# Gate units of attention in the first phase, output units of the convolution in the second: one decoder layer on one core

## The chip, the core and the metric

The kernel runs on one core of a Trainium2 chip. The core's engines work side by side, each through its own list of instructions in order: TensorE (PE, with PEld for its weight loads), VectorE (DVE), ScalarE (ACT), GpSimd (POOL) and SyncE (SP), which here only issues DMAs. An engine whose next instruction waits on a semaphore does nothing of what is queued behind it. The metric is the device time of one execution in microseconds.

## The reference

A decoder layer on 1024 tokens of width 1024 with two branches, all in float32. With h the normed and modulated input:

```python
proj = h @ w_in
(glu_a, glu_b, z_conv, q, k, v, z_att, g_conv, g_att) = jnp.split(proj, split_idx, axis=-1)

u = glu_a * sigmoid(glu_b)
u = causal_depthwise_conv(u, conv_w) + conv_b            # 31 taps, 1024 channels
u = silu(layernorm(u, conv_ln_g, conv_ln_b))             # over the channels
y_conv = (u * silu(z_conv)) @ w_conv_out

att = merged_dilated_window_attention(rope(q), rope(k), v)   # 3 groups of 8 heads
y_att = (att * silu(z_att)) @ w_att_out

merged = sigmoid(g_conv) * y_conv + sigmoid(g_att) * y_att
x = rmsnorm(x + gate * (merged @ w_o), final_g)
```

## The kernel before

Everything is kept transposed: 128 channels on the partitions, 1024 tokens along the free dimension; a whole such tile is 512 KB. A float32 product is made of three products of rounded parts (`mm3`, L72): each operand is split into a high part (ACT copy to fp32r) and a low part (a subtraction, mostly on POOL). `hh` and `hl` hold the parts of h for all eight channel tiles. A *unit* is 128 output columns of a weight matrix: 8 channel tiles x 2 token halves x 3 = 48 matmuls of 512 columns, done in four groups of 12.

**First phase (L400 to L1091).** A list `groups` holds one function of 12 matmuls per step. Beside it `todo` holds, for each step, the smaller jobs by rank: EARLY, COPY, EVICT, HIGH, POOLED, POST_, LOAD. The loop from L1060 writes out the instructions step by step in that order: EARLY, the group, ACT's work (COPY, EVICT, HIGH), POOL's, DVE's evictions (POST_), then `pump(GROUP)`, then what is left, DMA loads among it. `pump` gives 2.72 credits a step, at most 5.44 kept, to the generators in `behind`, DVE's long chains; each `yield` says what the piece just written costs (`GROUP, TAP, POST = 2.72, 1.33, 0.76`), and `spend` takes DVE's evictions off the same credit. This fixes the order in each engine's list; semaphores fix the times.

The steps before: 0 to 3 a plain unit, 4 to 19 v's second group (`values`), 20 to 131 sixteen *pairs*: two units as one Strassen product (`strassen`, L703) in seven groups instead of eight, with sums formed on POOL and, at its end, two sums on DVE (`summed`). Ten of the pairs are gates that go to scratch in DRAM after their activation (`Stored`). Then 132 to 147 v's third group in two turns, 148 to 155 the first two output units of the convolution together (`first_outputs`), and 156 to 179 the other six (`output`). A weight form of step s is copied by ACT at step s - 3 (`Form`, HIGH) and completed by POOL at step s - 2.

On DVE the depthwise convolution runs beside this, 31 taps for each of eight channel tiles (`conv`), each result stored to `vcscr`. Behind the last tap come the mean over channels by a matmul with ones (`norm_mean`), the squares (`norm_squares`), their column sums on PE and the reciprocal roots (`sums`, `scales`), the row of them by transposes (`rows`), then `norm_apply`: normalising, Silu, product with the stored gate z (`szscr`), and the split of u into parts `ch`, `cl`, which the output units read. The eight channel tiles `vt` stay in SBUF from the squares on. Then the rotation tables (`tables`), `ctab` and `stab`; the row sums of `w_ada` for the residual gate (`gate_sum`) lie between. `Gated` multiplies each output by the stored `gcscr` into `cscr`.

**Second phase (L1094 to L1607).** A loop over slots: each takes half of the contraction of a projection, 12 matmuls (`pieces`), beside stages of attention. 24 units are keys and queries (slots -11 to 84), rotated with the tables as they leave PSUM; then eight units of g_att, slots 85 to 116, which ACT copies out to `ascr` (`gate`). Attention's stages lie in slots 0 to 99, its merge (`combine`) up to slot 114. PSUM has two banks for the projections.

**Third phase.** For each d, `gates_load` reads `ascr` and `cscr`, ACT takes the Sigmoid of the first, and the output of attention is multiplied and added; the final product and norm follow.

Of the kernel before, what the change touches and what calls it, by code (L numbers as in the profile page):

```python
# [39 lines left out]
def layer(ctx: ExitStack, tc: tile.TileContext, a, out):  # L40
# [61 lines left out]
    vcscr = [dram.tile([P, S], F32, name=f"vcscr{j}") for j in range(KT)]  # L102
    szscr = [dram.tile([P, S], F32, name=f"szscr{j}") for j in range(KT)]
# [657 lines left out]
    ch, cl = [None] * KT, [None] * KT  # L761
    vt = [None] * KT
    row_of_mean = []

    def v_loads(cts):
        for ct in cts:
            vt[ct] = slot(f"t{ct}", f"vt{ct}")
            nc.sync.dma_start(vt[ct], vcscr[ct])
# [7 lines left out]

    def norm_squares():
        pm = row_of_mean[0]
        v_loads((KT - 1,))
        tot2 = slot("n2", "tot2")  # L780
        last = None
        for ct in range(KT):
            nc.vector.scalar_tensor_tensor(vt[ct], pm, -1.0 / D, vt[ct], op0=mult, op1=add)
            yield TAP
            sq = conv_in("sq")[:, 0:S] if ct else tot2
            nc.scalar.activation(sq, vt[ct], AF.Square)
            if last is not None:
                nc.vector.tensor_add(tot2, tot2, last)  # L788
# [3 lines left out]
        nc.vector.tensor_add(tot2, tot2, last)  # L792
        yield TAP

        def sums():
            pc = bank()[:, 0:8]
            col_sums(pc, tot2)
            at(now[0], POST_, lambda: scales(pc))
        at(now[0] + 1, EARLY, sums)

    def scales(pc):
        lcols = rstd_cols(pc, "l")
        nc.scalar.activation(one_b[:, 0:1], ones[:, 0:1], AF.Silu)

        def rows():
            lrow = acc_tile("lrow")
            for t in range(8):
                nc.tensor.transpose(lrow[:, t * P:(t + 1) * P], lcols[:, t:t + 1].to_broadcast([P, P]), ident)
            behind.append(norm_apply(lrow))
        at(now[0] + 1, EARLY, rows)  # L810

    sz_t = {}

    def sz_load(ct):
        sz_t[ct] = conv_in("sz")[:, 0:S] if ct % 4 < 2 else slot(f"n{1 + ct % 4}", "sz")
        nc.sync.dma_start(sz_t[ct], szscr[ct])

    def norm_apply(lrow):
        for ct in range(4):
            sz_load(ct)  # L820
        sg = [bank() for _ in range(2)]

        def scaled_mul(ct):
            nc.vector.tensor_mul(vt[ct], vt[ct], lrow)

        def scaled_(ct):
            scaled_mul(ct)
            silu(ct)

        def silu(ct):  # L830
            for half in range(2):
                nc.scalar.activation(sg[half], vt[ct][:, wide(half)], AF.Silu, scale=cvec[:, 1, ct:ct + 1],
                                     bias=cvec[:, 2, ct:ct + 1])

        scaled_(0)
        yield TAP
        for ct in range(KT):
            if ct + 1 < KT:
                scaled_mul(ct + 1)
                yield TAP  # L840
            for half in range(2):
                s = wide(half)
                nc.vector.tensor_mul(vt[ct][:, s], sg[half], sz_t[ct][:, s])
            yield 2 * POST
            if ct + 1 < KT:
                silu(ct + 1)
            hi, lo = slot(f"t{8 + ct}", f"uh{ct}", F32R), slot(f"t{ct - 1}" if ct else "n2", f"ul{ct}", F32R)
            nc.scalar.activation(hi, vt[ct], AF.Copy)
            ch[ct], cl[ct] = hi, lo
            at(now[0] + 1, POOLED, lambda ct=ct: nc.gpsimd.tensor_sub(cl[ct], vt[ct], ch[ct].bitcast(F32)))  # L850
            if ct + 4 < KT:
                sz_load(ct + 4)
# [7 lines left out]
    def tables():  # L860
        ctab, stab = (tabs[0].tile([P, S], F32, name=x) for x in ("ctab", "stab"))
        tabs.extend((ctab, stab))
        posi = pb.tile([P, S], I32, name="posi", tag="sd0")
        nc.sync.dma_start(posi, a["positions"].to_broadcast([P, S]))
        yield GROUP
        n_ = slot("sd1", "n_")
# [26 lines left out]
        yield from wrapped_sin(stab, slot("sd0", "m_"))  # L893
# [8 lines left out]
    class Gated:  # L902


        def __init__(self, step, d):
            self.d = d
            at(step, LOAD, self.load)

        def load(self):
            self.sg = slot(f"n{3 + self.d % 2}", "sgc")  # L910
            nc.sync.dma_start(self.sg, gcscr[self.d])

        def out(self, half, ps):
            y = piece("gs", "gs", 4)
            nc.vector.tensor_mul(y, ps, self.sg[:, wide(half)])
            spend(POST)
            nc.sync.dma_start(cscr[self.d][:, wide(half)], y)

    def gate_sum(step, d):
        box = []  # L920

        def load():
            box.append(slot("t7", "wada"))
# [7 lines left out]

    def u_block(kh, half):
        s = wide(half)
        return lambda k: (ch[4 * kh + k][:, s], cl[4 * kh + k][:, s])

    def first_outputs(step):
        raws = [Raw(step - 7 + 2 * d, a["w_co"][d]) for d in range(2)]
        forms = {(d, kh): Form(step + kh, raws[d].half(kh)) for kh in range(2) for d in range(2)}
        out = [Gated(step + 5, d) for d in range(2)]
        for d in range(KT):  # L940
            gate_sum(step + 7 + 3 * d, d)
        ps = {}

        def group(k):
            def fn():
                for d in range(2):
                    f = forms[d, k // 4]
                    c = slice(k % 4 * P, k % 4 * P + P)
                    for half in range(2):
                        if k == 0:  # L950
                            ps[d, half] = bank()
                        mm3(ps[d, half], f.hi[:, c], f.lo[:, c], ch[k][:, wide(half)], cl[k][:, wide(half)],
                            k == 0, k == KT - 1)
                if k == KT - 1:
                    for d in range(2):
                        for half in range(2):
                            at(now[0], POST_, lambda d=d, half=half: out[d].out(half, ps[d, half]))
            return fn
        return [group(k) for k in range(KT)]

    def output(step, d):
        raw = Raw(step - 6, a["w_co"][d])
        forms = [Form(step + 2 * i, raw.half(i)) for i in range(2)]
        out = Gated(step, d)
        ps = {}

        def group(i, half):
            def fn():
                if i == 0:
                    ps[half] = bank()  # L970
                block(ps[half], forms[i], u_block(i, half), i == 0, i == 1)
                if i:
# [785 lines left out]
```

## Time and profile before

| what | value |
| --- | --- |
| three runs | 1207.67, 1208.96, 1209.08 us; median 1208.96 |
| the profiled execution | 1208.01 us |
| its span, first to last instruction | 1206.2 us, granted clock 0.996 |
| DVE, ACT, POOL busy | 905.1, 586.7, 429.2 us |
| read from HBM, written | 122.25 MB, 39.62 MB |

How to read the views: a row of the groups gives line, engine, operation, output<-input with shape and count, then busy time and mean of one, then the idle time before it with what released it. A row of the order of time gives start and duration. A row of stretches gives for each engine the busy time and, in brackets, the number of instructions. An idle time matters only on the engine that sets the end.

### The profile page before, as it was taken

What the parts mean: (1) busy time and instruction counts of PE and PEld (TensorE: products, weight loads), DVE (VectorE), ACT (ScalarE), POOL (GpSimd) and SP (SyncE); (2) the same over time, 40 slices, a digit from 0 to 9 for tenths busy, and PEclk for the clock granted to TensorE, in tenths of its full rate; (3) what the DMA queues carried; (4) which work ended last, traced back from release to release, by engine and by line L of the source; (5) the groups of instructions that cost most, each with busy time, mean ns of one, the idle gap of its engine ahead of it and who ended that gap; (6) DMA issues with size and microseconds to landing.
All of it is one profiled execution on the core that took longest, in us unless ns stands there. A gap on an engine that the chain in (4) does not pass through costs nothing.

```text
span 1206.2 us, 17336 instructions
## 1 busy us (share of the span) xinstructions
PE 1189.1 (99%) x6042; PEld 996.1 (83%) x6042; DVE 905.1 (75%) x1488; ACT 586.7 (49%) x1213; POOL 429.2 (36%) x316
## 2 busy tenths in 40 slices
PE   9999999999999999999999999999999999999997
PEld 7787888888888888788888888888888888888886
DVE  7879999999999998796346657867877852649444
ACT  5655244545444443741126656656656664445111
POOL 0005867787787874672321111111111111200000
PEclk9999999999999999999999999999999999999999
DMA  9685333313233147666855455665666563768232
GB/s 358 192 300 175 105 106 122 101 66 105 100 100 131 63 140 274 226 201 235 225 135 149 111 144 130 181 174 141 180 168 146 145 191 124 234 228 281 87 105 70
DMA packets 100141, 194.49 MB, mean 161 GB/s; under 512 B 29587, under 2 KB 43219, under 8 KB 100054
## 3 DMA queue, kind: packets, MB, share of 16 engines
q1 hardware_dynamic: 83376, 186.77, 50.4%
q10 hardware_dynamic: 16678, 6.61, 2.0%
q8 instruction: 48, 0.79, 0.3%
q14 instruction: 39, 0.32, 0.1%
HBM read 122.25 MB, written 39.62 MB: 134 GB/s over the span
## 4 chain that ended last, share of the span: by engine, by line
PE 90%; DVE 3%; ACT 2%; DMA 2%; issue 1%; POOL 1%; SPq 0%; DVEq 0%; ACTq 0%; POOLq 0%
PE d L73 23%; PE d L74 23%; PE d L75 23%; PE o L1370 4%; PE d L603 4%; PE s L1333 3%; PE t L1349 3%; PE d L1661 2%; PE d L1662 2%; PE d L1663 2%; DMA wraw<-in_w_v 1%; PE d L274 1%; ACT hh L238 1%; DVE hl L241 1%; DVE tot L788 1%
## 5 line engine op out<-in xcount | busy, mean ns | idle before, releaser
L545 DVE SCALAR_TENSOR_TENSOR acc<-u,cw,acc 128x1024 f32<-128x1024 f32 x232 | 298.8, 1288 | 6.6
L73 PE MATMUL d<-hh,whi 128*128 128x512 f32 x752 | 295.0, 392 | 2.2 <-ACT gs L1023 2.2
L74 PE MATMUL d<-hl,whi 128*128 128x512 f32 x752 | 293.4, 390 | 0.0
L75 PE MATMUL d<-hh,wlo 128*128 128x512 f32 x752 | 293.3, 390 | 0.0
L456 POOL TENSOR_TENSOR wlo<-wraw,whi 128x512 fp32r<-128x512 f32 x130 | 175.8, 1362 | 216.4 <-ACT whi L453 216.2
L58 POOL TENSOR_TENSOR wlo<-wraw,whi 128x512 fp32r<-128x512 f32 (+1 forms) x56 | 82.9, 1498 | 366.5 <-ACT whi L57 362.5
L75 PEld LDWEIGHTS d<-hh,wlo 128*128 128x128 f32 x752 | 141.2, 188 | 30.2
L73 PEld LDWEIGHTS d<-hh,whi 128*128 128x128 f32 x752 | 141.4, 188 | 29.1 <-ACT gs L1023 2.7
L74 PEld LDWEIGHTS d<-hl,whi 128*128 128x128 f32 x752 | 141.4, 188 | 25.9
L453 ACT ACTIVATE whi<-wraw 128x512 fp32r<-128x512 f32 x130 | 79.1, 624 | 86.9 <-DMA wraw<-in_w_co 26.1
L1342 ACT ACTIVATE sb<-sb,stats 128x128 f32<-128x128 f32 (+1 forms) x192 | 84.8, 443 | 31.2 <-DVE stats L1338 30.9
L1338 DVE CUSTOM_DVE_ANT_0 sb<-s,mask 128x128 f32<-128x128 f32 (+1 forms) x192 | 59.7, 349 | 52.9 <-PE s L1333 51.5
L1349 PE MATMUL t<-ident,sb 128*128 128x128 f32 x280 | 73.7, 276 | 0.0
L1370 PE MATMUL o<-ph,vt 128*64 128x128 f32 (+1 forms) x432 | 65.9, 253 | 0.0
L1164 ACT ACTIVATE ph<-t 128x384 fp32r<-128x384 f32 (+2 forms) x96 | 45.6, 475 | 38.9 <-PE t L1349 25.8
L1167 DVE TENSOR_TENSOR pl<-t,ph 128x384 fp32r<-128x384 f32 (+2 forms) x96 | 52.0, 541 | 10.8 <-ACT ph L1164 10.2
L1333 PE MATMUL s<-k,ql 128*128 128x128 f32 (+1 forms) x192 | 55.0, 292 | 0.0
L1164 ACT ACTIVATE kqp<-rot 128x512 fp32r<-128x512 f32 x24 | 23.1, 964 | 64.4 <-DVE rot L1187 39.0
L1370 PE MATMUL o<-pl,vt 128*64 128x128 f32 (+1 forms) x216 | 52.8, 261 | 0.0
L1661 PE MATMUL d<-oh,hh 128*128 128x512 f32 (+1 forms) x136 | 51.2, 377 | 0.0
L1663 PE MATMUL d<-oh,hl 128*128 128x512 f32 (+1 forms) x136 | 51.2, 377 | 0.0
L73 PE MATMUL d<-uh,whi 128*128 128x512 f32 x128 | 50.0, 390 | 1.2 <-ACT gs L612 1.2
(300 smaller groups left out, 2640.2 us busy)
## 6 DMA issues: line engine op xcount, KB each, us to landing
wraw<-in_w_t SPq DMA_DIRECT2D x67, 512.0 KB, 4.2
k<-kqp SPq DMA_DIRECT2D x96, 128.0 KB, 2.3
q<-kqp SPq DMA_DIRECT2D x96, 128.0 KB, 2.3
wraw<-in_w_v SPq DMA_DIRECT2D x19, 512.0 KB, 4.5
wa<-in_w_ada SPq DMA_DIRECT2D x16, 512.0 KB, 5.8
ql<-kqp SPq DMA_DIRECT2D x48, 128.0 KB, 2.3
wg<-wscr SPq DMA_DIRECT2D x48, 128.0 KB, 3.2
hscr<-x SPq DMA_DIRECT2D x8, 512.0 KB, 3.4
```

Source lines behind the costliest of these rows:

```text
L58: (lo_eng or nc.vector).tensor_sub(lo, raw, hi.bitcast(F32))
L73: nc.tensor.matmul(ps, lh, rh, start=start, stop=False, skip_group_check=again)
L74: nc.tensor.matmul(ps, lh, rl, start=False, stop=False, skip_group_check=again)
L75: nc.tensor.matmul(ps, ll, rh, start=False, stop=stop, skip_group_check=again)
L453: nc.scalar.activation(self.hi, src(), AF.Copy)
L456: nc.gpsimd.tensor_sub(self.lo, src(), self.hi.bitcast(F32))
L545: nc.vector.scalar_tensor_tensor(acc, u[:, k:k + S], cw[:, ct, k:k + 1], acc, op0=mult, op1=add)
L1333: products.append((w, lambda c=c, w=w, l=x[:, ts_], r=k[:, ks], i=i: nc.tensor.matmul(ps[:, c:c + w], l, r, start=i == 0, stop=i == 1)))
L1342: nc.scalar.activation(sb[:, c:c + w], sb[:, c:c + w], AF.Exp, bias=stats[:, t, h, 1:2], scale=-1.0, accum_out=stats[:, t, h, 0:1])
L1349: yield from ((lambda c=c: nc.tensor.transpose(ps[:, c:c + P], sb[:, c:c + P], ident)) for c in range(0, o, P))
L1370: nc.tensor.matmul(out_, l, r, **kw))
L1661: nc.tensor.matmul(ps, hh[:, k, c], rh, start=k == 0, stop=False)
```

## The change

Attention's eight gate units become four Strassen pairs more (`GA`) in the first phase, steps 132 to 159, with their Sigmoid at once; v's third group moves to steps 160 to 175, and there the phase ends. The convolution's eight output units leave the first phase and take the gates' slots in the second, reading u from `hh` and `hl`, into which it is brought back from new scratch `uscr` once keys and queries have been projected. Because the Strassen tiles now stay in SBUF longer, the norm no longer keeps its channel tiles: `norm_squares` and `norm_apply` load them again. The core of the diff:

```diff
+    uscr = dram.tile([KT, P, S], F32, name="uscr")
...
+    def less_mean(v):
+        nc.vector.scalar_tensor_tensor(v, row_of_mean[0], -1.0 / D, v, op0=mult, op1=add)
+
+    def written_whole(step, ps):
+
+        at(step, EARLY, lambda: nc.tensor.matmul(ps, hh[:, 0, 0:P], hh[:, 0, 0:512], start=True, stop=True))
+
     def norm_squares():
-        pm = row_of_mean[0]
-        v_loads((KT - 1,))
+        d = {}
+
+        def load(ct):
+            d[ct] = conv_in("d")[:, 0:S] if ct % 3 < 2 else slot("n3", "d")
+            nc.sync.dma_start(d[ct], vcscr[ct])
+
+        for ct in range(3):
+            load(ct)
         tot2 = slot("n2", "tot2")
-        last = None
-        for ct in range(KT):
-            nc.vector.scalar_tensor_tensor(vt[ct], pm, -1.0 / D, vt[ct], op0=mult, op1=add)
+        yield 2 * GROUP
+
+        def square(ct):
+            less_mean(d[ct])
+            nc.scalar.activation(d[ct] if ct else tot2, d[ct], AF.Square)
+
+        square(0)
+        yield TAP
+        for ct in range(1, KT):
+            square(ct)
             yield TAP
...
+            if ct > 1:
+                nc.vector.tensor_add(tot2, tot2, d[ct - 1])
                 yield TAP
-            last = sq if ct else None
+            if ct + 2 < KT:
+                load(ct + 2)
...
-        at(now[0] + 1, EARLY, sums)
+        at(now[0] + 3, EARLY, sums)
...
         def rows():
-            lrow = acc_tile("lrow")
-            for t in range(8):
-                nc.tensor.transpose(lrow[:, t * P:(t + 1) * P], lcols[:, t:t + 1].to_broadcast([P, P]), ident)
+            lrow = slot("n4", "lrow")
+            for half in range(2):
+                pr = bank()
+                for t in range(4):
+                    nc.tensor.transpose(pr[:, t * P:(t + 1) * P],
+                                        lcols[:, 4 * half + t:4 * half + t + 1].to_broadcast([P, P]), ident)
+                nc.scalar.activation(lrow[:, wide(half)], pr, AF.Copy)
+                written_whole(now[0] + 1, pr)
             behind.append(norm_apply(lrow))
-        at(now[0] + 1, EARLY, rows)
+        at(now[0] + 2, EARLY, rows)
...
     def norm_apply(lrow):
...
+        v, z = {}, {}
+
+        def load(ct):
+            v[ct], z[ct] = conv_in("v")[:, 0:S], slot(f"n{2 + ct % 2}", "sz")
+            nc.sync.dma_start(v[ct], vcscr[ct])
+            nc.sync.dma_start(z[ct], szscr[ct])
+
+        def normed(ct):
+            less_mean(v[ct])
+            nc.vector.tensor_mul(v[ct], v[ct], lrow)
+            nc.scalar.activation(v[ct], v[ct], AF.Silu, scale=cvec[:, 1, ct:ct + 1], bias=cvec[:, 2, ct:ct + 1])
+
+        load(0)
+        load(1)
+        yield 2 * GROUP
+        normed(0)
+        yield 2 * TAP
         for ct in range(KT):
             if ct + 1 < KT:
-                scaled_mul(ct + 1)
-                yield TAP
...
+                normed(ct + 1)
+                yield 2 * TAP
+            nc.vector.tensor_mul(v[ct], v[ct], z[ct])
+            nc.sync.dma_start(uscr[ct], v[ct])
+            if ct + 2 < KT:
+                load(ct + 2)
+            yield TAP
...
     def gate_sum(step, d):
...
-            box.append(slot("t7", "wada"))
+            box.append(slot(f"t{d % 2}", "wada"))
...
+    GA = lambda n: stored_pair(60 + 2 * n, [ascr[2 * n], ascr[2 * n + 1]], S_[1])
     for make, n in ((glu_pair, 2), (SZ, 0), (glu_pair, 3), (SZ, 1), (glu_pair, 4), (ZA, 0), (glu_pair, 5), (ZA, 1),
-                    (SZ, 2), (glu_pair, 6), (GC, 0), (SZ, 3), (glu_pair, 7), (GC, 1), (GC, 2), (GC, 3)):
+                    (SZ, 2), (glu_pair, 6), (GC, 0), (SZ, 3), (glu_pair, 7), (GC, 1), (GC, 2), (GC, 3),
+                    *((GA, n) for n in range(4))):
         make(n)
-    at(len(groups), LOAD, lambda: v_loads(range(KT - 1)))
+    at(len(groups) + 1, LOAD, cb_load)
+    for d in range(KT):
+        gate_sum(len(groups) + 4 + d, d)
     for turn in range(2):
         take(values(len(groups), 2, turn))
-    at(len(groups) - 12, LOAD, cb_load)
-    take(first_outputs(len(groups)))
-    for d in range(2, KT):
-        take(output(len(groups), d))
...
-    def gate(d):
...
+    def gated(d, s):
+        y = ap_.tile([P, 512], F32, name="gc", tag="gs", bufs=2)
+        nc.sync.dma_start(y, gcscr[d][:, s])
+
+        def consume(ps):
+            nc.vector.tensor_mul(y, ps, y)
+            nc.scalar.dma_start(cscr[d][:, s], y)
         return consume
...
+        later = {0: ((prepare, kq + 1),), 1: ((raw_for, kq + 2),), 3: ((prepare, kq + 2), (raw_for, kq + 3))}
+        for n, (d, half) in enumerate([(0, 0), (1, 0), (0, 1), (1, 1)] + [(d, h) for d in range(2, KT) for h in range(2)]):
...
+    def u_back(kh, half):
+
+        for c in range(2):
+            k0 = 4 * kh + 2 * c
+            s = slice(half * 512, half * 512 + 512)
+            raw = tabs[0].tile([P, 2, 512], F32, name="u", tag=("ctab", "stab")[c])
+            nc.sync.dma_start(raw, uscr[k0:k0 + 2, :, s].rearrange("k p s -> p k s"))
+            raws["u", c] = raw
+        yield
+        for c in range(2):
+            k0 = 4 * kh + 2 * c
+            hi, lo, raw = hh[:, k0:k0 + 2, s], hl[:, k0:k0 + 2, s], raws["u", c]
+            nc.scalar.activation(hi, raw, AF.Copy)
+            (nc.vector if c else nc.gpsimd).tensor_sub(lo, raw, hi.bitcast(F32))
+        yield
...
+    for n, (kh, half) in enumerate(((0, 0), (1, 0), (0, 1), (1, 1))):
+        in_steps(u_back(kh, half), [80 + 2 * n, 82 + 2 * n])
...
         nc.sync.dma_start(sg_, ascr[d])
-        nc.scalar.activation(sg_, sg_, AF.Sigmoid)
         nc.sync.dma_start(tt, cscr[d])
```

`conv_in` has two buffers, the slots `n2`, `n3`, `n4` one each. `in_steps` runs a generator's first part (the load) at the first slot named and its second (the split) at the other. The table generator works in `ctab` itself and in `n2`, `n3` where it had slots of its own.

More of the change, by code (lines that the diff above doesn't have):

```diff
@@ L892, in tables @@
         yield from wrapped_sin(ctab, n_)
-        yield from wrapped_sin(stab, slot("sd0", "m_"))
+        yield from wrapped_sin(stab, slot("n3", "m_"))
         at(now[0] + 2, POST_, lambda: nc.vector.tensor_scalar(stab, stab, fr[:, 1:2], None, op0=mult))
@@ L930, in gate_sum @@
         at(step, POST_, post)
[L932 to L972, printed above, removed]
-                    at(now[0], POST_, lambda: out.out(half, ps[half]))
-            return fn
-        return [group(i, half) for i in range(2) for half in range(2)]
     groups = []
@@ L1596, in layer @@
                 next(c)
[L1597 to L1598 removed]
+            for do, u in prepared:
+                if u < units:
+                    do(u)
             if 0 <= slot_ < stages and st_ == 7:
```

105 lines of the change are left out of this document (29 added, 76 removed).

## The prediction

> **What bounds the kernel now.** I read the page first, then a table of stretches, then the two ends of the stretch that the change rewrites in TensorE's (PE's) order of time.
>
> ```profile
> span 1206.2 us, 17336 instructions
> ...
> PE 1189.1 (99%) x6042; PEld 996.1 (83%) x6042; DVE 905.1 (75%) x1488; ACT 586.7 (49%) x1213; POOL 429.2 (36%) x316
> ```
>
> PE is busy for 1189.1 of 1206.2 us, so time can fall only by giving PE less work or fewer waits, and any new wait of PE is added whole. The stretches (us; busy time of PE, PEld, DVE, ACT, POOL; granted clock; DMA) are: the block pairs of the first phase, its tail up to the first output of the convolution, the convolution's output units, and the second phase with attention.
>
> ```profile
> 99.00:459.00 360.00, 359.79 (x1584) 297.34 (x1585) 343.91 (x300) 157.99 (x266) 273.12 (x205) 1.00 0.33 108
> 459.00:510.90 51.90, 50.09 (x221) 40.30 (x219) 41.06 (x42) 30.64 (x47) 27.90 (x19) 0.97 0.73 263
> 510.90:598.80 87.90, 87.66 (x384) 72.03 (x385) 57.60 (x73) 25.29 (x37) 42.22 (x24) 1.00 0.70 230
> 598.80:1071.00 472.20, 472.20 (x2869) 407.85 (x2868) 304.06 (x803) 269.77 (x715) 80.90 (x60) 1.00 0.60 155
> ```
>
> PE is filled in all but the second, 459.0 to 510.9: there it lost time, and the clock was 0.97. That is where the layer norm of the convolution lies. In the pairs' stretch POOL is busy for 273 of 360 us and DVE for 344: four pairs more find room on POOL, and on DVE they come after its taps. PE's order of time (start, duration):
>
> ```profile
> 459.03 0.39 PE L603 MATMUL d<-whi,hh 128*128 128x512 f32 x1
> 459.26 0.39 PE L603 MATMUL d<-wlo,hh 128*128 128x512 f32 x1
> ...
> 472.63 1.88 PE L773 MATMUL pm<-tot,ones 128*128 128x512 f32 x4
> ```
>
> ```profile
> 510.91 0.50 PE L73 MATMUL d<-uh,whi 128*128 128x512 f32 x1 [1.22 <-ACT gs L612]
> ```
>
> ```profile
> 598.82 0.39 PE L73 MATMUL d<-hh,whi 128*128 128x512 f32 x1
> ```
>
> Starts are 0.227 us apart (459.26 less 459.03), though one row lasts 0.39: matmuls overlap, and the spacing is the price. One step of the first phase, 12 matmuls, is 2.72 us. Step 132 starts at 459.03 with v's last units; the mean of the norm (L773) comes five steps later, at step 137. Sixteen steps at 2.72 would end at 502.6; the first output unit started at 510.91, 8.4 us later, and the second phase at 598.82.
>
> **The change, part by part.**
>
> *Matmuls.* Step count of the first phase: 32 steps of output units go (8 of the first two, 24 of the rest), 28 steps of gate units come (four pairs of seven). The second phase keeps 32 units of 48 matmuls. PE saves 4 x 12 x 0.227 = **10.9 us**. Three filler matmuls (`written_whole`) add 0.7; the 4 + 4 transposes are the same eight as before. Of the 8.4 us lost in v's last units the mean's 1.9 (L773) stays, with sums and transposes at about 3.3 (my estimate); the rest could go, because more steps now lie between the norm's stages. Were that all, the phase would end 14.2 us earlier: 459.03 + 44 x 2.72 + 5.9 = 584.6.
>
> *The norm's first half* (`norm_squares`) now reloads v through three buffers. A reload waits for the sum two operations back, so a channel costs half of load, handover and two DVE operations (rows below): (3.7 + 0.3 + 2.4) / 2 = 3.2. Eight channels from 478 end near 504; the column sums come at step 149, 459.03 + 17 x 2.72 + 1.9 = 507.2. Hidden, with 3 us of cover; with loads of 5.1 it would be 1 us late.
>
> *The norm's second half.* Before, eight whole channels `vt` stayed in SBUF. Now `norm_apply` has two buffers for v and two for z, and each channel goes: load, less mean, times lrow, Silu, times z, store to `uscr`. Its order on DVE is normed(ct+1), then the product of ct, then the store of ct, then load(ct+2) into the buffer that this store reads. Load(ct+2) must therefore wait until the store of ct has landed, normed(ct+2) for that load, and the product of ct+1 stands behind normed(ct+2) on DVE. The chain runs through **every** channel, not every second one. That SP holds back a load until a store has landed shows here (SP's order of time, store and reload of the last channel):
>
> ```profile
> 470.39 0.33 SPq L560 DMA_DIRECT2D vcscr<-v  x1
> 480.12 0.33 SPq L768 DMA_DIRECT2D vt<-vcscr  x1
> ```
>
> The load was issued 9.7 us after the store, whose data it reads; a busy queue made that long. For a quiet queue: store of a channel, 512 KB, to landing (seven stores between 100 and 455 us, min/median/max), then loads of 512 KB of weights in the same stretch:
>
> ```profile
> DMA to landing us min/median/max: 2.6/3.2/6.0
> ```
>
> ```profile
> DMA to landing us min/median/max: 3.5/3.7/5.1
> ```
>
> The other terms, from the groups by shape between 459 and 603 us (busy, mean ns):
>
> ```profile
> L456 POOL TENSOR_TENSOR wlo<-wraw,whi 128x512 fp32r<-128x512 f32 x30 | 44.3, 1500 | 56.7 <-ACT whi L453 56.7
> ...
> L850 POOL TENSOR_TENSOR ul<-vt,uh 128x1024 fp32r<-128x1024 f32 x8 | 20.0, 2496 | 6.7 <-ACT uh L848 6.3
> L453 ACT ACTIVATE whi<-wraw 128x512 fp32r<-128x512 f32 x30 | 17.6, 622 | 38.9 <-DMA wraw<-in_w_co 26.1 <-DMA wraw<-in_w_v 9.7 <-POOL wlo L456 3.1
> ...
> L832 ACT ACTIVATE d<-vt,cvec 128x512 f32<-128x512 f32 x16 | 11.8, 773 | 3.9 <-DVE vt L824 3.6 <-DVE vt L843 0.2
> L915 DVE TENSOR_TENSOR gs<-d,sgc 128x512 f32<-128x512 f32 x16 | 10.7, 684 | 4.9 <-PE d L75 3.5 <-DMA sgc<-gcscr 1.3
> L843 DVE TENSOR_TENSOR vt<-d,sz 128x512 f32<-128x512 f32 x16 | 10.7, 687 | 3.0 <-ACT d L832 2.9
> L545 DVE SCALAR_TENSOR_TENSOR acc<-u,cw,acc 128x1024 f32<-128x1024 f32 x8 | 10.3, 1290 | 0.3
> L169 DVE CUSTOM_DVE_ANT_0 wada<-wada,cb 128x1024 f32<-128x1024 f32 x8 | 10.0, 1249 | 22.2 <-DMA wada<-in_w_ada 22.2
> L824 DVE TENSOR_TENSOR vt<-vt,lrow 128x1024 f32<-128x1024 f32 x8 | 9.6, 1212 | 3.9 <-PE lrow L808 3.9
> L783 DVE SCALAR_TENSOR_TENSOR vt<-pm,vt 128x1024 f32<-128x1024 f32 x8 | 9.5, 1214 | 2.9 <-PE pm L773 2.9
> ```
>
> DVE has three operations of 128x1024 per channel: 1.214 (L783), 1.212 (L824) and the product with z, unseen in that shape: between 1.21 like L824 and 1.37, twice L843; I take 1.21, the same shape and kind. With medians, a channel costs 3.2 + 3.7 + 3.64 + 0.3 for the handovers (my estimate; DVE to SP to DMA to DVE) = **10.8 us**; with the shortest and longest landings 9.7 to 15.
>
> *The Trainium skill*, "DMA: Bandwidth & Descriptors", section "Anatomy of one DMA — SWDGE (gpsimd) path", prices a DMA at about 2.0 us fixed plus bytes at 436 GB/s, which makes 3.2 us for 512 KB (for another queue than SP's). The trace has 3.2 for the store and 3.7 for the load. By the page the channel would cost 10.3 and the whole forecast 3 us less; I go by the rows.
>
> When does the chain start? I add up the credits that the planner's `yield` lines spend (2.72 given per step): mean at step 137 as before, column sums at 149, row at 151, loads 0 and 1 at 151, products of channels 0 to 7 at steps 154, 155, 157, 158, 160, 162, 163, 164, normed(7) at 162. Step 151 starts at 510.7 + 1.9 + about 2 for the sums, 514. With lrow copied by ACT (two halves) and four loads queued, normed(0) starts near 516.5 and the product of channel 0 ends near 523.5. The product of channel 5 ends 5 x 10.8 later, 577.5, and normed(7) 9.6 after that (10.8 less a product), 587.1.
>
> *What waits for it.* ACT runs its list in order. Silu(7) is issued in step 162, and the `high` copies of the weight forms stand behind it from step 163 on: those of step 166 and later. So step 166 cannot begin before 587.1 + 1.4 (Silu; two halves are 2 x 0.77, L832) + 0.6 (L453) + 1.5 (POOL, L456) = 590.6. SP is blocked by the same chain, and v's weight loads of steps 155 to 167 are behind its stores; GA's evictions on DVE too. Ten steps remain, 27.2 us: the phase ends at 617.8. PE idles before, so I add the 1.6 us that the granted clock of 0.97 cost in the first stretch above (3% of 51.9): **619.4**, against 598.8: +20.6 us. The saving of matmuls is inside this figure; it buys nothing, since the chain sets the end.
>
> *Tables and gate sums.* They follow on DVE. Tables (first and last operation):
>
> ```profile
> 523.75 1.49 DVE L867 CAST n__4233<-posi 128x1024 f32<-128x1024 int32 x1
> ...
> 564.01 0.74 DVE L894 TENSOR_SCALAR stab<-stab,fr 128x1024 f32<-128x1024 f32 x1
> ```
>
> That is 41 us, with other work and waits between. The operations themselves are one cast of 1.5, twelve with a constant at 0.74 (last row) and seven with two tensors at 1.21: 18.9 us. Eight gate sums are 8 x 1.25 (L169) plus small additions, 14 with an estimate of 0.5 each. From the product of channel 7 at 589.5 that gives 622 without any wait, 633 with half of the other 22 us. Phase two fills its two banks until 619.4 + 10.9 = 630.3 before it needs the rotation tables. Stall 0 to 6; I take **+2**.
>
> *Bringing u back (`u_back`).* Four quarters go one after the other through the two table buffers, while attention runs. Between slot 84's eviction and those of slots 86 and 88:
>
> ```profile
> 968.36 1.07 ACT L1164 ACTIVATE kqp<-d 128x512 fp32r<-128x512 f32 x1
> ...
> 975.46 0.57 ACT L1204 ACTIVATE gs<-d 128x512 f32<-128x512 f32 x1
> ...
> 985.67 0.58 ACT L1204 ACTIVATE gs<-d 128x512 f32<-128x512 f32 x1
> ```
>
> A quarter needs its load and then ACT, and POOL's 128x1024 subtraction, 2.5 us (L850): 3.6 in all. For the load a plain 512 KB stands above at 3.7; the one two-row gather of the same form is slower (page, issues; us to landing):
>
> ```profile
> traw<-hscr SPq DMA_DIRECT2D x8, 512.0 KB, 6.4
> ```
>
> With 5.0, between them, quarters are ready at 965, 974, 982, 991, against slots 85, 86, 89, 90 starting at 968, 972, 986, 989 (mean slot 472.2 / 128 = 3.7; the first load goes after slot 80's rotation, 957): a stall near 2, with 6.4 near 7, with 3.7 none. ACT and SP wait in order there too, with attention's exponentials behind them. I take **+4**, range 0 to 12.
>
> *At nothing:* the last units' eviction, a DVE product of 0.69 (L915) for ACT's copy, with 5.4 us until its bank is wanted; the stores of 256 KB stay, their loads have a unit's half to land. The eight Sigmoids of the last phase go from ACT, beside PE.
>
> Sum, from the profiled execution (1208.01: span 1206.2 and 1.8 around it; the median 1208.96 is 1 us more): 1208.0 + 20.6 + 2 + 4 = **1235 us**.
>
> **Rivals.**
>
> *The ring is hidden (faster).* If the two buffers overlapped loads with DVE, a channel would cost DVE's 3.64, the last product would end at 549, and neither SP nor ACT would hold PE. The phase ends at 584.6, tables at about 590, before their use at 595; 1208.0 - 14.2 + 4 = **1198**. For: the first two loads are early, and two steps are granted them. Against: the order written on DVE, with the reload behind the store. It decides at a channel cost of 6.6 us, where 523.5 + 6 x 6.6 + 29.5 meets 592.8 (598.8 less the 6 of later stalls); below it the kernel is faster. The Trainium skill, "Trainium Kernel Development and Optimization", section "Best Practices", says to double-buffer in order to overlap DMA with compute; by that rule this rival holds. No run here shows it for such a chain.
>
> *Nearly even.* Channel cost near 6.6: 1205 to 1211.
>
> *Later stalls are large.* The same chain, and `u_back` at 12 with attention held up, tables at 6 and landings nearer 6.0: above **1256**.
>
> **How the numbers follow.** Forecast 0.70 (own range 1216 to 1256), hidden ring 0.15, nearly even 0.06, large stalls 0.09. A measurement tells 0.2%, 2.4 us, from no change. Faster 0.16, same 0.05, slower 0.79. The range, 1206 to 1256, leaves out the hidden ring and part of the large stalls.
>
> **What would show it.** Right: SP waits in `norm_apply` for DMA `uscr`, eight products of z about 11 us apart, PE idle by over 30 us between 520 and 620 with a clock under 1, the second phase's first unit near 619. Wrong: products 4 us apart, PE filled, second phase near 585; then the ring's step fails. A start near 619 but another total puts the error on tables or `u_back`: PE waits behind hh or hl between slots 85 and 90.

## The result and the profile after

| | before | after |
| --- | --- | --- |
| median of four runs each, beside one another | 1209.02 us | 1286.84 us |
| all runs | 1207.67 to 1209.76 | 1285.38 to 1290.3 |
| profiled execution, its span | 1208.01, 1206.2 | 1285.38, 1283.6 |

The ratio is 1.0649, with a 95% interval of 1.0626 to 1.0673: slower by 78 us, where 26 were forecast. The direction and the chain of channels were right; the size lies far above the range. From the page of the kernel after (busy time; then the span in 40 slices):

```profile
span 1283.6 us, 17390 instructions
...
PE 1208.1 (94%) x5997; PEld 1004.9 (78%) x5997; DVE 933.2 (73%) x1500; ACT 608.0 (47%) x1238; POOL 460.4 (36%) x340
...
PE   9999999999999999676999999999999769989997
...
PEclk9999999999999999876999999999999879989999
```

PE has 45 instructions fewer than before (5997 against 6042) and is busy for longer: it ran part of them at a lower clock. The slices show two holes, at 510 to 610 us and at 990 to 1060, each with a dip of the clock, and a shallower third dip at 1123 to 1155, in the last phase. The stretches of the kernel after (us; busy time of PE, PEld, DVE, ACT, POOL; granted clock; DMA) say the same in numbers:

```profile
459.00:511.00 52.00, 50.75 (x226) 40.64 (x225) 36.01 (x29) 31.11 (x50) 39.09 (x28) 1.00 0.57 194
511.00:600.00 89.00, 60.74 (x217) 45.98 (x216) 32.55 (x34) 42.70 (x54) 25.14 (x20) 0.81 0.57 200
600.00:660.00 60.00, 54.62 (x218) 43.82 (x219) 46.31 (x58) 16.40 (x29) 32.33 (x24) 0.91 0.62 198
660.00:960.00 300.00, 300.00 (x1909) 261.33 (x1908) 213.14 (x589) 186.86 (x516) 49.03 (x38) 1.00 0.62 158
960.00:1060.00 100.00, 79.02 (x455) 66.93 (x454) 62.94 (x144) 52.03 (x131) 19.57 (x10) 0.86 0.62 166
```

No engine is near full in either hole; DVE, on which the chain of channels runs, is busy for only 32.6 of the 89 us from 511 on: this is waiting, not work. To see how much each hole costs, take instructions that both kernels have and subtract their starts. The second phase begins with a matmul of L73 (at 598.82 before, as shown above); attention's first and last exponential are ACT's, L1342 before and L1317 after. The kernel before:

```profile
633.88 0.41 ACT L1342 ACTIVATE sb<-sb,stats 128x128 f32<-128x128 f32 x1
...
1009.00 0.39 ACT L1342 ACTIVATE sb<-sb,stats 128x128 f32<-128x128 f32 x1
```

The kernel after, PE's order of time and then ACT's:

```profile
631.29 0.39 PE L73 MATMUL d<-hh,whi 128*128 128x512 f32 x1
```

```profile
673.04 0.41 ACT L1317 ACTIVATE sb<-sb,stats 128x128 f32<-128x128 f32 x1
...
1079.73 0.39 ACT L1317 ACTIVATE sb<-sb,stats 128x128 f32<-128x128 f32 x1
```

So the kernel is late by 32.5 us at the start of the second phase, by 39.2 at attention's first exponential, by 70.7 at its last, and by 77.4 at the end of the span. In the stretch from 660 to 960 PE is full: nothing is lost between the holes. These differences are the ledger by which every experiment below is read; each column holds what was lost since the mark before it (the second is 39.2 less 32.5), and the last their sum:

| us lost, against before | first phase | start of second | end of attention | last phase | span |
| --- | --- | --- | --- | --- | --- |
| forecast | 20.6 | 2 | 4 | 0 | 27 |
| after | 32.5 | 6.7 | 31.6 | 6.7 | 77.4 |

**The first hole.** DVE's products with z (L853) and, between two of them, the norm of the next channel but one:

```profile
529.12 1.23 DVE L853 TENSOR_TENSOR v<-v,sz 128x1024 f32<-128x1024 f32 x1 [1.29 <-ACT v L842]
541.24 1.22 DVE L772 SCALAR_TENSOR_TENSOR v<-pm,v 128x1024 f32<-128x1024 f32 x1 [10.89 <-DMA v<-vcscr]
542.50 1.22 DVE L841 TENSOR_TENSOR v<-v,lrow 128x1024 f32<-128x1024 f32 x1
543.64 1.22 DVE L853 TENSOR_TENSOR v<-v,sz 128x1024 f32<-128x1024 f32 x1
551.28 1.22 DVE L772 SCALAR_TENSOR_TENSOR v<-pm,v 128x1024 f32<-128x1024 f32 x1 [6.42 <-DMA v<-vcscr]
...
553.68 1.22 DVE L853 TENSOR_TENSOR v<-v,sz 128x1024 f32<-128x1024 f32 x1
...
587.58 1.22 DVE L853 TENSOR_TENSOR v<-v,sz 128x1024 f32<-128x1024 f32 x1
```

and SP's list beside them:

```profile
531.97 0.37 SPq L62 DMA_DIRECT2D wraw<-in_w_v  x1
532.43 0.39 SPq L854 DMA_DIRECT2D uscr<-v  x1
537.50 0.32 SPq L836 DMA_DIRECT2D v<-vcscr  x1
537.87 0.42 SPq L837 DMA_DIRECT2D sz<-szscr  x1
544.88 0.32 SPq L854 DMA_DIRECT2D uscr<-v  x1
547.49 0.32 SPq L836 DMA_DIRECT2D v<-vcscr  x1
```

The product of channel 1 ends at 544.86, the store goes out at 544.88, the reload behind it at 547.49, channel 3 is in its buffer at 551.28, and the product of channel 2 starts at 553.68, 10.04 us after the one before. From channel 1 to channel 5 a turn is (587.58 - 543.64) / 4 = 11.0 us. PE stands meanwhile; its largest waits in this phase, from the table of waits:

```profile
PE d L604 <- ACT whi L454: 10.1, 4, 4.0
...
PE d L73 <- ACT d L737: 9.5, 2, 9.3
```

These are weight copies and evictions on ACT, queued behind a Silu that waits for the chain. The last of them ends at the first matmul of step 166, the step that the prediction names (PE's order of time):

```profile
599.93 0.79 PE L604 MATMUL d<-whi,hh 128*128 128x512 f32 x1 [4.01 <-ACT whi L454]
```

**The second hole.** The gate of the convolution's second output unit, in all engines' order of time:

```profile
1042.38 1.14 SPq L1238 DMA_DIRECT2D q<-kqp  x2
...
1044.20 0.58 SPq L1146 DMA_DIRECT2D gc<-gcscr  x1
...
1047.71 0.69 DVE L1149 TENSOR_TENSOR gc<-d,gc 128x512 f32<-128x512 f32 x1 [8.91 <-DMA gc<-gcscr]
...
1048.44 0.34 ACTq L1150 DMA_DIRECT2D cscr<-gc  x1
...
1048.83 2.00 ACT L1226 ACTIVATE hh<-u 128x1024 fp32r<-128x1024 f32 x2 [9.26 <-DVE gc L1149]
```

and what PE waited for then (start, duration, idle time before it):

```profile
1049.94 0.80 PE L73 MATMUL d<-hh,whi 128*128 128x512 f32 x1 [9.39 <-ACT hh L1226]
```

Read it from the bottom: PE waits for `hh`, ACT's split of u stands behind its own DMA trigger, the trigger waits for DVE's product, the product for the gate, and SP issued the gate's load only at 1044.20, behind the last quarter of u and the moves of k and q. The forecast had this load at nothing.

### The profile page after: what moved, and what is told of

The parts are those of the page before. It is cut to its first block, busy times and chain, and to the rows that moved or that the text cites. A ratio compares the mean times of both kernels' runs of the same rounds, so it can differ in the third digit from the quotient of the medians.

```text
span 1283.6 us, 17390 instructions
## 1 busy us (share of the span) xinstructions
PE 1208.1 (94%) x5997; PEld 1004.9 (78%) x5997; DVE 933.2 (73%) x1500; ACT 608.0 (47%) x1238; POOL 460.4 (36%) x340
## 5 line engine op out<-in xcount | busy, mean ns | idle before, releaser
L73 PE MATMUL d<-hh,whi 128*128 128x512 f32 x800 | 317.7, 397 | 15.3 <-ACT hh L1226 9.4
L75 PE MATMUL d<-hh,wlo 128*128 128x512 f32 x800 | 315.8, 395 | 5.9 <-POOL wlo L58 5.9
L74 PE MATMUL d<-hl,whi 128*128 128x512 f32 x800 | 315.2, 394 | 2.4 <-POOL hl L1227 2.4
L73 PEld LDWEIGHTS d<-hh,whi 128*128 128x128 f32 x800 | 152.3, 190 | 45.3 <-ACT hh L1226 9.6
L75 PEld LDWEIGHTS d<-hh,wlo 128*128 128x128 f32 x800 | 152.0, 190 | 39.7 <-POOL wlo L58 7.2
L74 PEld LDWEIGHTS d<-hl,whi 128*128 128x128 f32 x800 | 152.1, 190 | 31.8 <-POOL hl L1227 3.2
L1317 ACT ACTIVATE sb<-sb,stats 128x128 f32<-128x128 f32 (+1 forms) x192 | 84.8, 443 | 38.8 <-DVE stats L1313 38.7
L1313 DVE CUSTOM_DVE_ANT_0 sb<-s,mask 128x128 f32<-128x128 f32 (+1 forms) x192 | 59.7, 349 | 52.3 <-PE s L1308 51.1
L604 PE MATMUL d<-whi,hh 128*128 128x512 f32 x128 | 53.8, 421 | 12.4 <-ACT whi L454 10.1
L457 POOL TENSOR_TENSOR wlo<-s,whi 128x512 fp32r<-128x512 f32 x40 | 51.7, 1293 | 29.4 <-ACT whi L454 29.4
L604 PE MATMUL d<-wlo,hh 128*128 128x512 f32 x128 | 54.5, 425 | 3.3 <-POOL wlo L457 3.3
L604 PE MATMUL d<-whi,hl 128*128 128x512 f32 x128 | 53.4, 417 | 0.0
L1345 PE MATMUL o<-pl,vt 128*64 128x128 f32 (+1 forms) x216 | 53.1, 262 | 0.0
```

Of the source, the lines that this page charges most:

```text
L73: nc.tensor.matmul(ps, lh, rh, start=start, stop=False, skip_group_check=again)
L74: nc.tensor.matmul(ps, lh, rl, start=False, stop=False, skip_group_check=again)
L75: nc.tensor.matmul(ps, ll, rh, start=False, stop=stop, skip_group_check=again)
L457: nc.gpsimd.tensor_sub(self.lo, src(), self.hi.bitcast(F32))
L604: nc.tensor.matmul(ps[i], l[:, k, c], r, start=k == 0 and n == 0, stop=k == KT - 1 and n == 2)
L1313: nc.vector.tensor_tensor_reduce(out=sb[:, c:c + w], in0=ps[:, c:c + w], in1=mk, scale=-SCALE, scalar=3e38, op0=add, op1=ALU.min, accum_ou ...
```

## The experiments

Each kernel is the one after with the edit shown. The table has, in us against the kernel before, the same ledger; the text gives the device times. A figure of one run is marked so. How far one run can be read is seen where an edit leaves the code of a column alone: the first phase then lies between 30.2 and 34.3 (five kernels), the end of attention between 30.0 and 31.6 and the last phase between 6.6 and 8.6 (five each); whole times of one kernel spread by up to 6 us.

| kernel | first phase | start of second | end of attention | last phase | span |
| --- | --- | --- | --- | --- | --- |
| e4_gates_silu | 29.5 | 7.0 | 31.4 | 8.6 | 76.6 |
| e1b_order | 23.9 | 7.5 | 30.0 | 6.8 | 68.2 |
| e9_zprod | 14.4 | 5.8 | 30.0 | 8.0 | 58.3 |
| e11_no_apply | -4.9 | 1.1 | 31.2 | 6.6 | 34.1 |
| e2_no_gate_load | 30.4 | 9.6 | 20.5 | 0.0 | 60.5 |
| e3_no_u_back | 34.3 | 6.8 | 3.4 | 8.6 | 53.1 |
| e8_gate_early | 32.5 | 6.7 | 17.8 | 2.8 | 59.7 |
| e7_sub_pool | 30.2 | 9.5 | 27.8 | 6.3 | 73.7 |
| e10_all | 14.1 | 6.7 | 18.6 | 4.4 | 43.9 |
| e12_all_early | 9.1 | 9.4 | 15.9 | 6.4 | 40.8 |
| e13_neither | -7.0 | 0.0 | 3.4 | 3.2 | -0.4 |

**The first phase: tables on ACT.**

```diff
-    GA = lambda n: stored_pair(60 + 2 * n, [ascr[2 * n], ascr[2 * n + 1]], S_[1])
+    GA = lambda n: stored_pair(60 + 2 * n, [ascr[2 * n], ascr[2 * n + 1]], S_[0])
```

> The attention's gate units are evicted with Silu in place of Sigmoid, so ACT changes no table between them and the norm's Silus; the gate's values differ, everything else is done. Theory A (some 12 table loads of 1.28 us between 506 and 582 delay the start of the ring by 5 to 7 us, and hardly its period): first z product near 523 instead of 529, period 11 us, time 1276 to 1281 us. Rival B (ACT's table loads stand beside the ring): within 2 us of 1285. Rival C (they are part of the period too): 1270 or less.

One run: 1284.69 us, the first product at 530.4, though from 505 to 582 us ACT loads a table 4 times instead of 14. Rival B holds. In the kernel after the start was late for another reason, seen in DVE's order of time but not tried by itself:

```profile
516.63 0.20 DVE L114 RECIPROCAL ltmp<-ltmp 128x8 f32<-128x8 f32 x1 [5.39 <-ACT ltmp L113]
...
522.24 0.69 DVE L633 TENSOR_TENSOR gs<-d,sd 128x512 f32<-128x512 f32 x1 [2.92 <-PE d L75]
522.85 1.21 DVE L772 SCALAR_TENSOR_TENSOR v<-pm,v 128x1024 f32<-128x1024 f32 x1
```

The norm's root stood on ACT for 5.4 us, and the first channel's norm stood on DVE behind an eviction that waited 2.9 for PE.

**The first phase: the order of the chain.**

```diff
-            if ct + 1 < KT:
-                normed(ct + 1)
             nc.vector.tensor_mul(v[ct], v[ct], z[ct])
             nc.sync.dma_start(uscr[ct], v[ct])
             if ct + 2 < KT:
                 load(ct + 2)
+            if ct + 1 < KT:
+                normed(ct + 1)
```

> The z product, its store and the reload of channel ct+2 are written ahead of the norm of channel ct+1; nothing else differs and the result is the same. Theory A (the ring through every channel sets the end of the first phase): the product of ct+1 no longer stands behind the norm of ct+2, so store 3.2 + load 3.7 + two DVE operations 2.4 + Silu 1.5 + product 1.2 + 0.3 = 12.3 us now covers two channels; the eight z products stand about 6 us apart instead of 11.5, the last starts near 573 instead of 601, the first phase ends some 25 us earlier and the time is about 1260 us (1250 to 1270). Rival B (ACT, which changes between Silu and Sigmoid, or the granted clock sets the end): products still 10 us or more apart, time 1280 to 1290.

The granted clock stood near 0.75 in this run from its first slice to its last, so its time of 1517.36 us is not used.

> The same kernel as e1_order, run again: that run had a granted clock of 0.75 from its first to its last slice, so its time says nothing; in it the z products stood 8.7 us apart, with a store that took 2.9 to 7.7 us until the next load could start. Theory A (the ring through every channel sets the end of the first phase): at full clock the products stand 6 to 9 us apart, the last of them starts at 575 to 592 instead of 601, the first phase ends at 604 to 621 instead of 630.6, time 1260 to 1277. Rival B (something else sets the end): the phase ends within 4 us of 630.6, time 1281 or more.

1279.4 us (1276.47 and 1282.34), the second phase at 622.7: between the two. Products at 530.55 and, six turns later, at 579.60: 8.2 us a turn instead of 11, so the order alone is worth 8.6 us of the first phase; a turn stays above the 6.2 of the expectation's terms. The last product comes 15.8 us after the seventh.

With this order kept, the product goes to z's buffer:

```diff
-            nc.vector.tensor_mul(v[ct], v[ct], z[ct])
-            nc.sync.dma_start(uscr[ct], v[ct])
+            nc.vector.tensor_mul(z[ct], v[ct], z[ct])
+            nc.sync.dma_start(uscr[ct], z[ct])
```

> As e1_order, and the product is written into z's buffer and stored from there, so the reload of v no longer waits for the store; only the reload of z does. Same result. Theory A (the store leg is the larger part of what is left of the ring): products 5 to 7 us apart, the first phase ends 5 to 15 us before that of e1b_order, time 1250 to 1268. Rival B (SP holds its queue in order, so that the next store and the next v stand behind z's reload, which waits for the same store): within 3 us of e1b_order.

1266.05 us (1265.55 and 1266.55). Theory A: products 6.9 us apart (529.12 to 570.25 in six turns), the phase 9.5 us shorter than in e1b_order. DVE's order of time in e9_zprod shows the first and the seventh product, and where the last one went:

```profile
529.12 1.23 DVE L850 TENSOR_TENSOR sz<-v,sz 128x1024 f32<-128x1024 f32 x1 [3.67 <-ACT v L842]
...
570.25 1.23 DVE L850 TENSOR_TENSOR sz<-v,sz 128x1024 f32<-128x1024 f32 x1 [1.37 <-ACT v L842]
...
575.53 1.23 DVE L841 TENSOR_TENSOR v<-v,lrow 128x1024 f32<-128x1024 f32 x1
583.25 1.78 DVE L170 CUSTOM_DVE_ANT_0 wada<-wada,cb 128x1024 f32<-128x1024 f32 x1 [6.50 <-DMA wada<-in_w_ada]
...
585.19 1.22 DVE L850 TENSOR_TENSOR sz<-v,sz 128x1024 f32<-128x1024 f32 x1
```

A gate sum waits for its weights with the last product behind it. With one cause gone, the next in line holds the phase.

**The first phase without the chain.** The loads, the norm, Silu and the product go; eight copies from `vcscr` to `uscr` stand in their place.

> Leaves out the second half of the convolution's norm: no loads, norm, Silu or product of channels; eight copies from one place in device memory to another put v where u would be. The rest of the changed kernel stays. Theory A (the chain of channels is all of the first phase's loss): without it the first phase ends at 585 to 595 instead of 630.6, which the prediction had as 584.6 for a hidden chain; the second phase still loses its 31 us at the end, time 1238 to 1251. Rival B (the gate sums, tables and weight loads of the phase's last steps hold it as well): it ends at 600 or later, time 1256 or more.

One run: 1242.13 us. The second phase's first matmul, in PE's order of time of e11_no_apply:

```profile
593.92 0.39 PE L73 MATMUL d<-hh,whi 128*128 128x512 f32 x1
```

Theory A: the chain costs 37.4 us of the first phase and 5.6 of the start of the second, 43 in all; the end of attention loses the same 31 us at any start.

**The second phase: the gate's load.**

```diff
-        nc.sync.dma_start(y, gcscr[d][:, s])
...
-            nc.vector.tensor_mul(y, ps, y)
+            nc.scalar.activation(y, ps, AF.Copy)
```

> Leaves out the product with the convolution's gate: an output unit of the convolution in the second phase is copied out of its bank by ACT and stored, and the gate is not loaded. Theory A (the gate load stuck in SP's queue holds the DVE product, the product holds ACT's store trigger, and ACT's split of u waits behind it): of the 28 us that the second phase loses between the evictions of slots 82 and 92, 15 or more go, time 1258 to 1270 us. Rival B (u_back's loads and splits alone are late): less than 8 go, time 1279 to 1287.

One run: 1268.57 us; 11.1 us go at the end of attention and 6.7 in the last phase, so theory A's total holds, though 11.1 is less than the 15 it named, and 20.5 stay. u's return has a cost of its own.

**The second phase: u's return.** `u_back` isn't called, `hh` and `hl` keep h.

> Leaves out bringing u back: the output units of the convolution multiply h, which stays in hh and hl, instead of u. All matmuls, gate loads, products and stores stay. Theory A (the loss needs both, the gate load behind u's loads on SP and the split of u behind the product on ACT): all but 5 of the 28 us go, time 1256 to 1264 us. Rival B (the gate loads are late for another reason, the buffers of tag gs or the moves of k and q): 10 us or more stay between slots 82 and 92, time 1267 to 1285.

One run: 1261.13 us. Attention's first and last exponential, in ACT's order of time of e3_no_u_back:

```profile
674.97 0.40 ACT L1317 ACTIVATE sb<-sb,stats 128x128 f32<-128x128 f32 x1
...
1053.52 0.40 ACT L1317 ACTIVATE sb<-sb,stats 128x128 f32<-128x128 f32 x1
```

378.55 us lie between them, 375.12 in the kernel before (633.88 to 1009.00): theory A, 3.4 us are left.

**The gate kept, but early.** Its load goes one unit ahead; the trigger of the store goes to the next slot:

```diff
-            nc.scalar.dma_start(cscr[d][:, s], y)
+            lows.append(lambda: nc.scalar.dma_start(cscr[d][:, s], y))
...
+                if after and 0 < n < 2 * KT - 1:
+                    gate_load(*outs[n + 1])
```

`gate_load` issues the load that stood in `gated`; the first two go out ahead of the last projection of keys and queries.

> The gate of a convolution output unit is loaded one unit earlier (ahead of u's loads on SP), and ACT's trigger of the store stands one slot later, behind the u split. Same result. Theory A (the gate load stuck on SP and the trigger stuck on ACT are what e2_no_gate_load took away): the second phase loses about 21 us between slots 82 and 92 as there, not 31.6, and the start of the last phase is not held, time 1266 to 1274. Rival B (leaving DVE's product out was the gain there): 1279 or more.

One run: 1267.65 us, theory A, and no worse at the end of attention than without the product (17.8 against 20.5): it was the place in the queues, not the work. The 9.4 us wait for `hh` is gone from PE's waits. Among what is left, in PE's order of time of e8_gate_early:

```profile
1008.67 0.45 PE L1335 MATMUL t<-ident,sb 128*128 128x128 f32 x1 [4.50 <-DVE pl L1110]
```

That is attention waiting for its low parts, behind u's on DVE.

```diff
-            (nc.vector if c else nc.gpsimd).tensor_sub(lo, raw, hi.bitcast(F32))
+            nc.gpsimd.tensor_sub(lo, raw, hi.bitcast(F32))
```

> Both low parts of a quarter of u are subtracted on POOL; before, DVE did one of the two, for which it stood idle 3.5 us and then worked 2.5 us with attention's low parts behind it. Same result. Theory A (attention waits behind u's low part on DVE): the 4.5 us wait of PE for DVE pl at 1008 goes; POOL now takes 4.8 us for a quarter instead of 2.4, so PE waits for POOL hl grow by up to 2.4 each; time 1280 to 1287. Rival B (the low parts are not on the path): the wait for DVE pl stays.

One run: 1281.83 us, theory A. PE's waits for DVE's `pl` fall from 5.5 us to 0.7, those for POOL's `hl` grow from 2.4 to the 7.8 of its table, and the end of attention gains 3.8:

```profile
PE d L74 <- POOL hl L1227: 7.8, 7, 1.9
```

**All together.**

> e9_zprod, e8_gate_early and e7_sub_pool in one kernel; same result as the reference. If the three causes stand one behind the other in time (first phase 20.6 us, gate loads and triggers 19, DVE's low part 4 to 5), their gains add up: 1266.0 - 19 - 4.5 = 1243 (1239 to 1248). If what one sets free is taken up by the next in line, 1250 or more.

1252.53 us (1251.91 and 1253.15): the gains don't add up. Those of the first phase and of the early gate do; POOL's is gone, for the end of attention loses 18.6 us against 17.8 with the early gate alone.

```diff
-        in_steps(u_back(kh, half), [80 + 2 * n, 82 + 2 * n])
+        in_steps(u_back(kh, half), [80 + 2 * n, 81 + 2 * n])
...
-        gate_sum(len(groups) + 4 + d, d)
+        gate_sum(len(groups) + 8 + d, d)
```

> e10_all, with the split of each quarter of u one slot after its load instead of two, and the gate sums four steps later, behind the chain of channels (in e9_zprod the last product stood 7.7 us behind a gate sum that waited for its weights). Same result. Theory A (a quarter's turn, load and split, is what is left of the loss in the second phase, some 13 us after e10_all): 5 to 10 us of it go and the first phase ends 4 to 8 us earlier, time 1226 to 1236. Rival B (the quarters' loads land too late for an earlier split, ACT stands and attention with it): 1240 or more. Nothing here reaches the kernel before unless the first phase ends below 600.

1249.57 us (1248.74 to 1250.68; ratio 1.034, interval 1.0323 to 1.0358). The first phase did end 5 us earlier, but of u's loss only 2.7 us went, and 4.7 came back at the start of the second and in the last phase: rival B. ACT's order of time in e12_all_early has the load that lands too late:

```profile
999.86 1.06 ACT L1237 ACTIVATE hh<-u 128x1024 fp32r<-128x1024 f32 x1 [3.46 <-DMA u<-uscr]
```

PE's shows the next wait in line:

```profile
1001.92 0.79 PE L73 MATMUL d<-hh,whi 128*128 128x512 f32 x1 [5.70 <-ACT whi L57]
...
1005.71 0.79 PE L75 MATMUL d<-hh,wlo 128*128 128x512 f32 x1 [2.57 <-POOL wlo L58]
```

Now the next unit's weights wait on ACT and POOL behind u's parts.

**Neither chain nor u.** e11_no_apply, e3_no_u_back and e8_gate_early in one.

> Leaves out both the second half of the convolution's norm (as e11_no_apply) and bringing u back (as e3_no_u_back), with the gates loaded early as in e8_gate_early. What is left of the change is the move of the units: 48 matmuls less in the first phase, the gate products, the gate sums and the tables. Theory A (the chain of channels, u_back and the late gates are the whole loss): attention begins 4 us before the kernel before (as in e11_no_apply), loses 0 to 4 us at its end, and the time is 1203 to 1212, level with the kernel before or up to 0.4% faster. Rival B (the move costs something of its own): 1218 or more.

1210.0 us (eight runs, 1207.63 to 1213.73; ratio 1.0017, interval 1.0002 to 1.0033): theory A. With both costs out the move of the units is level with the kernel before. None of the kernels tried beats it.

## Why the prediction was right or wrong

- **Matmuls, 10.9 us saved: right, and worth less than the hidden rival had it.** Without the chain the second phase starts at 593.92 (e11_no_apply) or 591.78 (e13_neither), not at 584.6; in the latter 3.4 us more are lost at the end of attention and 3.2 in the last phase. The rival of 1198 stood on a floor that the kernel doesn't reach: with the chain wholly gone it runs in 1242, with u's return gone too in 1210.
- **The norm's first half, hidden: right.** The last sum of squares was there at 507.3, and PE came to it at 509.2 without a wait. (By the prediction's own terms loads of 5.1 would have made it 2 us late, not 1.)
- **The chain of channels: mechanism right, size short.** Product 0 was forecast to end at 523.5 and ended at 530.35 (6.9 late); the first turn took 14.5 us (529.12 to 543.64), since the store of channel 0 went out 2.1 us after its product (532.43) and the reload followed 5.1 later (537.50); turns 2 to 5 took 11.0 against 10.8. From product 5's end (588.80) to the second phase it took 42.5, against 41.9 forecast. The terms that were mis-sized are the start, 6.9, and the first turn, 3.7: queues on ACT, DVE and SP ahead of the first channels were not priced. (The lower bound of a turn, 9.7, leaves out the 0.3 of the handovers that the upper one has; with it the bound is 10.0.) The rule to double-buffer (the Trainium skill, "Trainium Kernel Development and Optimization", section "Best Practices"), on which the hidden rival stood, is not borne out by two buffers alone: 11.0 us a turn, and 6.9 with another order and the store taken from another buffer (e9_zprod).
- **The clock, 1.6 us: too small.** The forecast carried the 0.97 of before over; it fell to 0.81 and 0.91 in the stretches above. Where the term was added, in the ten steps behind the chain, PE took 31.4 us (599.93 to 631.29) for the 27.2 that were counted; 0.8 of it is a wait for POOL, so the clock cost some 3.3 there (an estimate from these rows). For u's return no such term was set: from 960 to 1060 PE stood for 21.0 us, and its 79.0 busy us at a clock of 0.86 are 11.1 more than at 1.00, together 32.1 beside the ledger's 31.6. This too is an estimate from the rows; no run changes the clock alone.
- **Tables and gate sums, +2: right as named, incomplete.** PE's wait for the rotation was 2.0 us; with another of 2.6 for POOL's weight part and matmuls at the lower clock behind it (last section) that makes 6.0 of the 6.7. The sum of 18.9 for the tables was a misreading: in the kernel before, four of the twelve operations with a constant took 1.7 to 2.8 us, and all twenty 24.5.
- **u's return, +4 with 12 as the upper end: the step that failed.** It was priced as a pipeline of its own, load, ACT, POOL, and the end of attention lost 31.6. What the runs show is what stands in the same queues: the late gate load and the trigger behind it (13.8 us, e8_gate_early), attention's low parts behind u's on DVE (3.8 by itself, e7_sub_pool, and nothing more beside early gates, e10_all), and the rest gone only when u isn't brought back (e3_no_u_back). The sentence "ACT and SP wait in order there too" was in the text and had no price.
- **"At nothing", the last units' eviction: wrong.** "Their loads have a unit's half to land" counted the landing, not when SP would come to issue them. In the last phase PE's wait for the last product, 3.8 us, fell to 0.3 in e8_gate_early; what the whole column gains by it stays open, for it stands at 2.8 in e8_gate_early and at 6.4 in e12_all_early, which has them too.
- **The signs named beforehand** held in kind, not all in size: SP's waits for `uscr`, 16.0 us in six (below), the product of z every 11 us, a clock of 0.81, and the later error as a wait behind `hh` between slots 85 and 90. PE idled by 27.6 us from 520 to 620, where over 30 were named, and the second phase began at 631.3, not near 619.

```profile
SPq L836 <- DMA uscr<-v: 16.0, 6, 4.6
```

Taken together: of the 77.4 us (77.5 by the rounded columns), 43 are the chain's, 28.2 those of u's return with the late gates (31.6 less 3.4), and 6.3 are left: 3.4 at the end of attention and 6.7 in the last phase, less the 3.8 by which attention begins earlier without the chain.

## What to carry to other kernels

A step that is moved into a busy stretch costs what its instructions wait for, and what then stands behind them in each engine's list: price every DMA issue and trigger by its place in the queue, not by its landing time. Two buffers overlap nothing when the next channel's first instruction stands ahead of this channel's last one and its load behind this channel's store. And where a cost is taken out, the next wait in line takes part of the gain: try the edits together before adding up their gains.

## What was not expected of the hardware

After a wait of 2.56 us PE ran at half rate for 3 us, then at full rate (PE's order of time after; spacing 0.42, then 0.22):

```profile
634.46 0.74 PE L75 MATMUL d<-hh,wlo 128*128 128x512 f32 x1 [2.56 <-POOL wlo L58]
635.01 0.63 PE L73 MATMUL d<-hh,whi 128*128 128x512 f32 x1
635.43 0.63 PE L74 MATMUL d<-hl,whi 128*128 128x512 f32 x1
...
637.99 0.39 PE L74 MATMUL d<-hl,whi 128*128 128x512 f32 x1
638.21 0.40 PE L75 MATMUL d<-hh,wlo 128*128 128x512 f32 x1
```

The Trainium skill, "TensorE: Matmul & The Clock Gate", section "HAM oscillation — how this bites in real kernels", gives the rule that PE should have no idle gap above about 3.4 us. Here a shorter one was followed by half rate, and the measurement decides: this wait cost some 1.4 us on top of its own 2.56 (seven matmuls from 635.01 to 637.57, each 0.2 us longer), with a granted clock of 0.53 from 634.4 to 638.0. The length of one wait does not settle it: in the same trace a wait of 1.98 us before 1025.65, shortly behind one of 1.73, was followed by a clock of 0.55 for 5.4 us, and one of 2.01 before 648.78 by 1.00. What decides between them stays open.
